# Own buffers for the memory's raw weights, and new durations for transfers, ScalarE and GpSimd in the list scheduler

## The chip, the cores and the metric

The kernel runs on one core of a Trainium2 chip. Five engines of that core run their own instruction streams in order: TensorE (matrix products, called PE in the profile, with its weight loads as PEld), VectorE (DVE), ScalarE (ACT), GpSimd (POOL) and SyncE (SP). In this kernel every transfer between the chip's main memory and the on-chip memory (SBUF) is issued from SP's queue, and is then carried out by 16 transfer engines. Products land in PSUM, which has 8 banks; VectorE and ScalarE read them from there. The metric is the device time of one execution in microseconds, lower is better.

## The reference

One inference step of one layer of a streaming encoder, for 1024 prompt rows and 32 sample rows, width 1024, all in 32-bit floats:

- p = RMSNorm(x) @ w_in. Half of the columns feed an HGRN2 mixer (4 heads, a gated linear recurrence computed in blocks), the other half an RWKV-7 mixer (8 heads, a delta-rule recurrence computed in chunks of 64).
- x = x + concat(HGRN2, RWKV7) @ w_out.
- Cross attention: the memory (256 rows) is normalised and turned into keys and values, mk = RMSNorm(mem) @ w_ck and mv = RMSNorm(mem) @ w_cv, which are also outputs. The sample rows use cached keys and values instead. x = x + softmax(q mk^T / 16) mv @ w_co, with q from w_cq.
- x = x + (silu(n @ w_ff1) * (n @ w_ff3)) @ w_ff2 with 2816 hidden columns, and a last RMSNorm.

Outputs are the normalised rows, the new recurrence states, the last projected rows, and the memory's keys and values.

## The kernel before

The kernel is written in two layers. Class Net calls operations on a recorder (class Graph). Each call becomes a node with an engine, a price in microseconds, predecessors, and the tiles (class Buf) it touches; runs of matmuls up to a cut form one node. Then Graph.order (line 376) is a list scheduler that runs while the program is being built: it keeps a clock for every engine, takes again and again the node that can start first, prefers on one engine the node with the longest remaining path, and gives every new tile an address. The order it finds is what each engine then runs, in order, on the chip. All instructions are emitted from line 365, which is why the profile shows one line for all of them, and tiles there carry the name of the memory region they were put in.

Prices come from `price` (line 218): a duration, which occupies the engine, and a second value, `late`, which delays the successors only. For a transfer the duration occupies SP in the plan.

The SBUF is cut into regions (line 59), counted in units of 66 floats a partition: f0 (192 units), wr (32), r0 (256), rw (64), mb (192) and ma (64). Regions mb and ma change from plain 32-bit tiles to tiles of rounded parts once few enough mixer nodes are left. HOME (line 64) binds some tile classes to regions; a plain class that is not in HOME may go to any plain region but wr, and its tile is given out only if a reserve of units stays free (RESERVE, line 61; 32 units for phase 1). FIFO (line 69) limits how many tiles of a class live at one time, and tiles of a class in FIFO are handed out in program order.

Every matrix product against weights is done with both operands split into a rounded high part and a low remainder. `load_w` (line 764) loads the raw weights with one transfer of 512 KB, casts the high part on ScalarE, subtracts on VectorE or GpSimd for the low part, and three products follow for each block. Its raw tile is of class "wr" (2 alive, region wr), high and low parts are of classes "wh" and "wl" (2 alive each, region rw).

Work is in phases: 0 the two mixers with their projections, 1 the memory's keys and values (`memory_kv`, line 886), 2 the output projection, 3 cross attention, 4 the hidden layer of the feed-forward part, 5 and 6 its output and the last norm. LEAD (line 63) says how many nodes of earlier phases may be left when a phase starts; it is 1100 for phase 1. Phase 1 has the lowest priority of all (bias of 2e5 on the path), so that it fills gaps. It loads 16 half weights of 512 rows by 256 columns, 8 of w_ck and 8 of w_cv, and each one serves 24 products of 256 columns: 2 row tiles, 4 blocks, 3 products. The normalised memory rows lie in region ma, so that in the profile these products read "rw,ma".

Of the kernel before, what the change touches and what calls it, by code (L numbers as in the profile page):

```python
# [11 lines left out]
F32 = mybir.dt.float32  # L12
# [4 lines left out]
ALU = mybir.AluOpType  # L17
# [48 lines left out]
        "ac": ("f0", "ma"), "hst2": ("f0", "ma"), "fu": ("f0", "ma")}  # L66

TASTE = [{"f0": 0.0, "wr": 0.0, "r0": 0.0, "rw": 0.0, "mb": 20.0, "ma": 10.0}, {"f0": 20.0, "wr": 0.0, "r0": 0.0, "rw": 0.0, "mb": 0.0, "ma": 10.0}]
FIFO = {"wr": 2, "wh": 2, "wl": 2, "p": 44, "rp": 5, "op": 32, "sr": 2, "sh": 4, "sx": 4, "sh3": 8, "hst2": 4, "xr": 2, "wr2": 4, "wh2": 8, "wl2": 8, "ckv": 7, "mrow": 2}

INDEX = (np.arange(128, dtype=np.int64)[:, None] << 20) + np.arange(8 * 1056, dtype=np.int64)[None]

# [145 lines left out]
def price(eng, method, args, kw):  # L218

    out = args[0] if args else kw.get("out")  # L220
    n = math.prod(out.shape[1:]) if out is not None and hasattr(out, "shape") else 1
    if method == "dma_start":
        return max(0.4, n * out.shape[0] * 4 / 200e3), 1.9
    if eng == "tensor":
        if method == "transpose":
            return (0.056 if args[1].shape[0] <= 64 else 0.109), 0.0
        lhs = kw["lhsT"]
        k, m = lhs.shape[0], math.prod(lhs.shape[1:])
        if lhs.dtype == F16:
            return max(0.029, n / 2400 + 0.002), 0.0  # L230
        if lhs.dtype == F32R:
            return (n if n >= 256 else 4 * n) * 0.4375e-3 + 0.007, 0.0
        if k <= 64 and m <= 64:
            return max(0.03, n * 0.92e-3), 0.0
        if k <= 64:
            return max(0.112, n * 1.25e-3), 0.0
        if m <= 64:
            return (0.059 if n >= 64 else 0.112), 0.0
        return max(0.223, n / 600 + 0.005), 0.0
    if eng == "vector":  # L240
        if method == "tensor_reduce":
            n = math.prod(args[1].shape[1:])
        if method == "tensor_tensor_scan":
            return 0.07 + n * 2.08e-3, 0.0
        return 0.065 + n * 1.05e-3 + (0.065 if method == "scalar_tensor_tensor" else 0.0), 0.0
    if method == "preload_act_table_set":
        return 1.28, 0.0
    if eng == "scalar":
        pointer = any(isinstance(kw.get(k), View) for k in ("scale", "bias", "accum_out"))
        return (0.18 if args[1].buf.space == "PS" else 0.21) + n * 0.83e-3 + (0.095 if pointer else 0.0), 0.0  # L250
    if method == "affine_select":
        return 0.35, 0.0
    if method == "memset":
        return 0.06 + n * 0.5e-3, 0.0
    if method == "tensor_tensor":
        return 0.13 + n * 2.12e-3 + (0.45 if args[3] == ALU.pow else 0.0), 0.0
    if method == "tensor_scalar":
        return 0.3 + n * (2.9e-3 if args[4] == ALU.max else 1.3e-3), 0.0
    return 0.24 + n * 1e-3, 0.0


def shares_port(eng, method, args):
# [22 lines left out]
class Graph:  # L285
    def __init__(self, ctx, tc):
# [5 lines left out]
        for name in ("vector", "scalar", "gpsimd", "tensor", "sync"):  # L292
            setattr(self, name, Engine(self, name))
        self.bufs = {c: [] for c in FIFO}

# [26 lines left out]
    def record(self, eng, method, args, kw):  # L322
        if eng == "tensor" and self.open is not None:
            node = self.open
        else:
            node = Node(self, eng)
        self.open = node if eng == "tensor" else None
        cost, late = price(eng, method, args, kw)
        node.port = shares_port(eng, method, args)
        node.cost, node.late = node.cost + cost, max(node.late, late)  # L330
        node.calls.append((method, args, kw))
        node.dense = method == "matmul" and kw["lhsT"].dtype == F32R
        for at, a in list(enumerate(args)) + list(kw.items()):
            if isinstance(a, View):
                a.buf.touch(node, a, at in (0, "out", "accum_out"))
        if method == "activation" and args[2] in (AF.Exp, AF.Ln, AF.Tanh, AF.Sigmoid):
            if self.fence is not None:
                node.preds[self.fence] = None
            self.table.append(node)
        if method == "preload_act_table_set":  # L340
            node.preds.update(dict.fromkeys(self.table))
            self.fence = node
        return node
# [32 lines left out]
    def order(self):  # L376
# [84 lines left out]
        banks = [0.0] * 8  # L461
        turn, live = dict.fromkeys(FIFO, 0), dict.fromkeys(FIFO, 0)
        done, oldest, out = set(), 0, []
# [26 lines left out]
        def fits(n, start):  # L490
# [7 lines left out]
            if not new:  # L498
                return start
            for c in FIFO:  # L500
                k = sorted(b.turn for b in new if b.cls == c)
                if k and (k != list(range(turn[c], turn[c] + len(k))) or live[c] + len(k) > FIFO[c]):
                    return None
# [19 lines left out]
        def take(n, start):  # L523
            for b in sorted((b for b in n.bufs if b.at is None and b.fixed is None), key=lambda b: -b.units):
# [8 lines left out]
                freed[b.at:b.at + b.units] = BIG  # L533
                if b.cls in FIFO:
                    turn[b.cls] += 1
# [9 lines left out]
        while len(done) < len(nodes):  # L545
# [48 lines left out]
            for b in n.bufs:  # L594
                b.left -= 1
                if not b.left and b.fixed is None:
# [3 lines left out]
                    else:  # L600
                        freed[b.at:b.at + b.units] = end + FREE_SB
                        if b.cls in FIFO:
                            live[b.cls] -= 1
# [16 lines left out]
class Net:  # L620
# [140 lines left out]
        return self.par[:, at + j:at + j + n]  # L761


    def load_w(self, ap, nk, gain=None, m=128, small=False, eng=None):

        nc = self.nc
        size, tag = (nk, "2") if small else (1024 // m, "")
        raw = self.wp.tile([128, size, m], F32, tag="wr" + tag, name="wraw")[:, :nk]
        nc.sync.dma_start(raw, ap.rearrange("(k p) m -> p k m", p=128))
        hi = self.wp.tile([128, size, m], F32R, tag="wh" + tag, name="whi")[:, :nk]  # L770
        if gain is not None:
            nc.vector.tensor_tensor(raw, raw, gain.unsqueeze(2).to_broadcast([128, nk, m]), ALU.mult)
        nc.scalar.copy(hi, raw)
        lo = self.wp.tile([128, size, m], F32R, tag="wl" + tag, name="wlo")[:, :nk]
        (eng or nc.vector).tensor_tensor(lo, raw, hi.bitcast(F32), ALU.subtract)
        return hi, lo
# [109 lines left out]
    def memory_kv(self):  # L886

        nc = self.nc
        mh = self.ap.tile([128, KD, 256], F32R, name="mh")
        ml = self.ap.tile([128, KD, 256], F32R, name="ml")  # L890
        rs = self.load_rows([(self.i["mem_prompt"][0, 128 * a:128 * a + 128, :], 128, 128 * a) for a in range(2)], mh, ml, None,
                            lambda: self.ap.tile([128, 512], F32, tag="mrow", name="mrow"), self.P("g_mem", 0, KD))
        for h in range(4):
            for key, out in (("w_ck", self.mk), ("w_cv", self.mv)):
                pss = [self.psg.tile([128, 256], F32, tag="g", name="ps_mem") for _ in range(2)]
                for a in range(2):
                    hi, lo = self.load_w(self.i[key][0, 512 * a:512 * a + 512, 256 * h:256 * h + 256], 4, m=256,
                                         eng=nc.vector)
                    for t, ps in enumerate(pss):
                        ts = slice(128 * t, 128 * t + 128)  # L900
                        nc.cut()
                        for k in range(4):
                            mm = partial(nc.tensor.matmul, ps)
                            mm(lhsT=mh[:, 4 * a + k, ts], rhs=hi[:, k], start=a + k == 0, stop=False)
                            mm(lhsT=mh[:, 4 * a + k, ts], rhs=lo[:, k], start=False, stop=False)
                            mm(lhsT=ml[:, 4 * a + k, ts], rhs=hi[:, k], start=False, stop=a == 1 and k == 3)
                for t, ps in enumerate(pss):
                    nat = self.ap.tile([128, 256], F32, tag="nat", name="nat")
                    nc.scalar.activation(nat, ps, AF.Copy, scale=rs[:, t:t + 1])
                    nc.sync.dma_start(out[:, t, h], nat)  # L910
# [982 lines left out]
```

## Time and profile before

| | us |
|---|---|
| median of 3 runs | 1973.01 |
| lowest and highest run | 1971.82, 1973.35 |
| span of the profiled execution, first to last instruction | 1970.2 |
| TensorE busy in it | 1873.7 |
| VectorE busy | 1403.0 |
| ScalarE busy | 837.8 |
| GpSimd busy | 657.9 |

The page shows busy time of each engine, then 40 slices of the span with the busy share in tenths, the granted TensorE clock in tenths, and the busy share of the transfer engines. A timeline row has start, length, engine, line, operation, out<-in by region, shape and count, and in brackets the idle time before it with what ended that. "DMA f<-out_dram" as a releaser means that the engine waited for that transfer to land. A row of SPq is the issue of a transfer, not its duration.

### The profile page before, as it was taken

How to read it: one execution, taken by the hardware profiler on the slowest of the kernel's cores; microseconds unless marked ns; L12 is line 12 of the kernel's file. 1: busy time of each engine (PE TensorE's matmuls, PEld its weight loads, DVE VectorE, ACT ScalarE, POOL GpSimd, SP SyncE). 2: the span in 40 equal slices, each digit the busy share in tenths (PEclk: the TensorE clock that was granted, in tenths of full speed). 3: DMA queues.
4: the chain of work that ended last, by engine and by line, in shares of the span. 5: the costliest groups of instructions: out<-in, count | busy, mean ns of one | idle time of the engine just before them, and what ended most of it. 6: DMA issues, size and time to landing. Idle time of an engine off the chain costs nothing. (4 is left out here: it accounts for less than half of the span.)

```text
span 1970.2 us, 40636 instructions
## 1 busy us (share of the span) xinstructions
PE 1873.7 (95%) x15785; PEld 1733.5 (88%) x15785; DVE 1403.0 (71%) x3112; ACT 837.8 (43%) x2151; POOL 657.9 (33%) x926
## 2 busy tenths in 40 slices
PE   6899999999999999799999999899999999999998
PEld 6788888887888888699899999799999999999997
DVE  4787789568957876524555446797777877968997
ACT  4553545454545455533322235533323323464432
POOL 4632444235425432104500003633332333322421
PEclk8899999999999999799999999899999999999999
DMA  4100110011001102551112112222223224455632
GB/s 143 38 7 26 41 40 23 7 50 38 13 28 45 34 18 69 155 156 43 43 43 70 39 60 88 71 82 93 82 100 129 88 83 137 138 181 170 183 90 89
DMA packets 158111, 149.51 MB, mean 76 GB/s; under 512 B 10080, under 2 KB 146400, under 8 KB 157920
## 3 DMA queue, kind: packets, MB, share of 16 engines
q1 hardware_dynamic: 157920, 146.93, 23.7%
q8 instruction: 124, 2.03, 0.4%
q14 instruction: 67, 0.55, 0.1%
HBM read 111.02 MB, written 35.88 MB: 75 GB/s over the span
## 5 line engine op out<-in xcount | busy, mean ns | idle before, releaser
L365 PE MATMUL bank<-r,rw 128*128 128x264 f32 (+1 forms) x5808 | 928.4, 310 | 28.8 <-DVE rw L365 10.6
L365 PEld LDWEIGHTS bank<-r,rw 128*128 128x128 f32 x5808 | 824.6, 190 | 49.1 <-DVE rw L365 12.2
L365 PE MATMUL bank<-mb,rw 128*128 128x264 f32 (+3 forms) x3456 | 484.5, 293 | 10.4 <-DVE rw L365 8.9
L365 PEld LDWEIGHTS bank<-mb,rw 128*128 128x128 f32 x3456 | 455.5, 189 | 19.5 <-DVE rw L365 13.5
L365 DVE TENSOR_TENSOR f<-bank,f 128x264 f32<-128x264 f32 (+11 forms) x798 | 317.5, 421 | 121.2 <-PE bank L365 114.9
L365 PE MATMUL bank<-f 64*64 64x64 f32 (+8 forms) x2472 | 281.6, 258 | 36.1 <-DVE f L365 17.5
L365 PEld LDWEIGHTS bank<-f 64*64 64x64 f32 (+5 forms) x1675 | 169.3, 157 | 73.0 <-DVE f L365 22.4
L365 ACT CAST rw<-wr 128x1024 fp32r<-128x1024 f32 (+3 forms) x183 | 132.8, 730 | 224.7 <-PE bank L365 138.7
L365 POOL TENSOR_TENSOR f<-f 128x2 f32<-128x2 f32 (+9 forms) x167 | 106.2, 648 | 317.3 <-ACT f L365 241.0
L365 ACT ACTIVATE f<-f 128x256 f32<-128x256 f32 (+7 forms) x392 | 158.0, 423 | 114.1 <-DVE f L365 88.1
L365 DVE TENSOR_TENSOR f<-f 128x264 f32<-128x264 f32 (+10 forms) x266 | 187.7, 719 | 24.3 <-POOL f L365 12.0
L365 DVE TENSOR_TENSOR rw<-wr,rw 128x512 fp32r<-128x512 f32 (+3 forms) x153 | 129.4, 850 | 81.4 <-ACT rw L365 80.6
L365 ACT COPY f<-bank 128x264 f32<-128x264 f32 (+6 forms) x251 | 87.6, 361 | 119.1 <-PE bank L365 104.6
L365 ACT CAST rw<-ma 128x512 fp32r<-128x512 f32 (+2 forms) x124 | 70.9, 573 | 153.2 <-POOL ma L365 85.8
L365 DVE TENSOR_TENSOR rw<-ma,rw 128x512 fp32r<-128x512 f32 (+2 forms) x124 | 82.5, 672 | 35.2 <-ACT rw L365 35.0
L365 POOL TENSOR_SCALAR f<-f 128x64 f32<-128x64 f32 (+6 forms) x117 | 49.2, 422 | 165.0 <-DVE f L365 104.7
L365 PE MATMUL bank<-f,mb 64*64 64x64 f32 (+9 forms) x982 | 84.5, 241 | 3.8 <-DVE f L365 2.4
L365 ACT ACTIVATE f<-bank,f 128x256 f32<-128x256 f32 (+4 forms) x127 | 52.6, 430 | 73.8 <-DVE f L365 32.4
L365 ACT CAST f<-bank 128x256 f16<-128x256 f32 (+1 forms) x144 | 46.5, 339 | 87.8 <-PE bank L365 56.9
L365 POOL TENSOR_TENSOR ma<-ma 128x512 f32<-128x512 f32 (+4 forms) x41 | 53.4, 1304 | 90.5 <-DVE rw L365 90.1
L365 POOL TENSOR_TENSOR ma<-wr 128x512 f32<-128x512 f32 (+1 forms) x13 | 25.1, 1928 | 161.6 <-DVE rw L365 95.2
L365 DVE TENSOR_TENSOR f<-bank,r 128x264 f32<-128x264 f32 (+1 forms) x56 | 25.2, 465 | 71.2 <-PE bank L365 64.2
(189 smaller groups left out, 2233.2 us busy)
## 6 DMA issues: line engine op xcount, KB each, us to landing
wr<-in_w_in_dram SPq DMA_DIRECT2D x30, 512.0 KB
wr<-in_w_ff_dram SPq DMA_DIRECT2D x27, 512.0 KB
ma<-in_w_ff_dram SPq DMA_DIRECT2D x25, 512.0 KB
h_scratch<-f SPq DMA_DIRECT2D x18, 528.0 KB
f<-h_scratch SPq DMA_DIRECT2D x36, 264.0 KB
ma<-h_scratch SPq DMA_DIRECT2D x34, 264.0 KB
h_scratch<-f SPq DMA_DIRECT2D x12, 396.0 KB
f<-mix_scratch SPq DMA_DIRECT2D x24, 176.0 KB
```

The lines of the kernel that those rows point to most:

```text
L365: getattr(eng, method)(*args, **kw)
```

## The change

The raw tiles of the memory's weights become a class of their own, "wm", with up to 6 alive; "wm" is not in HOME. Class "wr" keeps its 2 tiles for all other weights. The high and low parts stay in "wh" and "wl". In `price`, the duration of a transfer falls from bytes/200e3 to bytes/330e3 us (its `late` of 1.9 stays), ScalarE's fixed part falls from 0.18 (source in PSUM) and 0.21 (source in SBUF) to 0.06 and 0.11 while it gets a `late` of 0.1, and GpSimd's prices of affine_select, memset, tensor_scalar and the remaining operations change. Prices of TensorE, VectorE and GpSimd's tensor_tensor stay.

```diff
-FIFO = {"wr": 2, "wh": 2, "wl": 2, "p": 44, "rp": 5, ...
+FIFO = {"wm": 6, "wr": 2, "wh": 2, "wl": 2, "p": 44, "rp": 5, ...
...
     if method == "dma_start":
-        return max(0.4, n * out.shape[0] * 4 / 200e3), 1.9
+        return max(0.4, n * out.shape[0] * 4 / 330e3), 1.9
...
-        return (0.18 if args[1].buf.space == "PS" else 0.21) + n * 0.83e-3 + (0.095 if pointer else 0.0), 0.0
+        return (0.06 if args[1].buf.space == "PS" else 0.11) + n * 0.83e-3 + (0.095 if pointer else 0.0), 0.1
     if method == "affine_select":
-        return 0.35, 0.0
+        return 0.38, 0.0
     if method == "memset":
-        return 0.06 + n * 0.5e-3, 0.0
+        return 0.1 + n * 0.8e-3, 0.0
     if method == "tensor_tensor":
         return 0.13 + n * 2.12e-3 + (0.45 if args[3] == ALU.pow else 0.0), 0.0
     if method == "tensor_scalar":
-        return 0.3 + n * (2.9e-3 if args[4] == ALU.max else 1.3e-3), 0.0
-    return 0.24 + n * 1e-3, 0.0
+        return 0.2 + n * (3.4e-3 if args[4] == ALU.max else 1.05e-3), 0.0
+    return 0.16 + n * 1e-3, 0.0
...
-    def load_w(self, ap, nk, gain=None, m=128, small=False, eng=None):
+    def load_w(self, ap, nk, gain=None, m=128, small=False, eng=None, early=False):
...
-        raw = self.wp.tile([128, size, m], F32, tag="wr" + tag, name="wraw")[:, :nk]
+        raw = self.wp.tile([128, size, m], F32, tag="wm" if early else "wr" + tag, name="wraw")[:, :nk]
...
                     hi, lo = self.load_w(self.i[key][0, 512 * a:512 * a + 512, 256 * h:256 * h + 256], 4, m=256,
-                                         eng=nc.vector)
+                                         eng=nc.vector, early=True)
```

More of the change, by code (lines that the diff above doesn't have):

```diff
@@ L68 @@
 TASTE = [{"f0": 0.0, "wr": 0.0, "r0": 0.0, "rw": 0.0, "mb": 20.0, "ma": 10.0}, {"f0": 20.0, "wr": 0.0, "r0": 0.0, "rw": 0.0, "mb": 0.0, "ma": 10.0}]
-FIFO = {"wr": 2, "wh": 2, "wl": 2, "p": 44, "rp": 5, "op": 32, "sr": 2, "sh": 4, "sx": 4, "sh3": 8, "hst2": 4, "xr": 2, "wr2": 4, "wh2": 8, "wl2": 8, "ckv": 7, "mrow": 2}
+FIFO = {"wm": 6, "wr": 2, "wh": 2, "wl": 2, "p": 44, "rp": 5, "op": 32, "sr": 2, "sh": 4, "sx": 4, "sh3": 8, "hst2": 4, "xr": 2, "wr2": 4, "wh2": 8, "wl2": 8, "ckv": 7, "mrow": 2}
 INDEX = (np.arange(128, dtype=np.int64)[:, None] << 20) + np.arange(8 * 1056, dtype=np.int64)[None]
```

## The prediction

> **What bounds the kernel now.** I read the page's busy shares and slices first, then busy time by stage, then the timeline of the one weak stage engine by engine, and last the group rows for prices.
>
> ```profile
> span 1970.2 us, 40636 instructions
> PE 1873.7 (95%) x15785; PEld 1733.5 (88%) x15785; DVE 1403.0 (71%) x3112; ACT 837.8 (43%) x2151; POOL 657.9 (33%) x926
> PE   6899999999999999799999999899999999999998
> PEclk8899999999999999799999999899999999999999
> DMA  4100110011001102551112112222223224455632
> ```
>
> TensorE is the bound: 1970.2 - 1873.7 leaves 96.5 us without a matmul. The seventeenth slice (788 to 837 us) is the one dent in the middle, for the engine and for its granted clock, and the transfer engines are at their mid-run peak there. The stages, as busy time of each engine, granted clock, transfer share, GB/s:
>
> ```profile
> 0.00:160.00 160.00, 133.06 (x1130) 119.09 (x1131) 110.00 (x246) 81.76 (x205) 79.33 (x172) 0.91 0.21 65
> 160.00:600.00 440.00, 429.00 (x4385) 364.32 (x4383) 327.77 (x910) 220.30 (x683) 172.56 (x331) 1.00 0.10 28
> 600.00:781.00 181.00, 177.75 (x1876) 149.90 (x1873) 130.28 (x386) 89.29 (x289) 69.64 (x128) 1.00 0.12 36
> 781.00:866.00 85.00, 68.25 (x474) 62.19 (x472) 42.55 (x92) 45.07 (x103) 10.30 (x23) 0.86 0.57 178
> 1160.00:1320.00 160.00, 147.29 (x1136) 143.92 (x1136) 117.52 (x218) 76.92 (x180) 62.70 (x58) 0.96 0.26 84
> 1700.00:1850.00 150.00, 143.41 (x1145) 141.52 (x1144) 123.80 (x215) 76.41 (x165) 45.88 (x38) 0.99 0.55 166
> 1850.00:1971.00 121.00, 111.40 (x860) 107.17 (x858) 106.33 (x252) 40.03 (x104) 30.98 (x55) 0.98 0.34 108
> 500.00:550.00 50.00, 47.18 (x570) 39.66 (x569) 43.64 (x115) 22.18 (x67) 21.36 (x42) 1.00 0.04 13
> ```
>
> The 85 us in which the last mixer head ends and the memory keys and values are made lose 85 - 68.25 = 16.75 us. Opened up on TensorE (start, length, tiles, count, idle time before and what ended it):
>
> ```profile
> 786.72 6.26 PE L365 MATMUL bank<-rw,ma 128*128 128x256 f32 x48
> 793.87 9.09 PE L365 MATMUL bank<-f 128*128 128x128 f32 x59 [0.89 <-DVE f L365]
> 805.15 0.28 PE L365 MATMUL bank<-f 128*32 128x128 f32 x1 [2.18 <-DVE f L365]
> 806.06 2.98 PE L365 MATMUL bank<-f 128*32 128x32 f32 x10 [0.63 <-DVE f L365]
> 810.56 0.31 PE L365 MATMUL bank<-f 32*128 32x32 f32 x1 [1.52 <-ACT f L365]
> 810.80 14.40 PE L365 MATMUL bank<-rw,ma 128*128 128x256 f32 x96
> 830.25 1.11 PE L365 MATMUL bank<-f 128*128 128x128 f32 x4 [5.05 <-DMA f<-out_dram]
> 834.74 0.58 PE L365 MATMUL bank<-rw,ma 128*128 128x256 f32 x1 [3.38 <-ACT rw L365]
> 836.00 17.05 PE L365 MATMUL bank<-rw,ma 128*128 128x256 f32 x120 [0.68 <-DVE rw L365]
> 853.93 5.95 PE L365 MATMUL bank<-rw,ma 128*128 128x256 f32 x48 [0.88 <-DVE rw L365]
> ```
>
> The rows "rw,ma" are the memory products, 24 to one loaded half weight. They are meant as filler for the mixers' last dependent steps, but three halves are eaten by 793 and the fourth is not there until 810.8, so 0.89, 2.18, 0.63 and 1.52 us (5.22) stay open. Then 5.05 and 3.38 (8.43) wait on transfers. What the transfer queue and ScalarE did meanwhile:
>
> ```profile
> 787.18 0.38 SPq L365 DMA_DIRECT2D wr<-in_w_cv_dram  x1
> 792.40 0.43 SPq L365 DMA_DIRECT2D wr<-in_w_ck_dram  x1
> 815.19 10.76 SPq L365 DMA_DIRECT2D f<-mix_scratch  x12
> 826.00 0.42 SPq L365 DMA_DIRECT2D f<-out_dram  x1
> 826.47 0.46 SPq L365 DMA_DIRECT2D wr<-in_w_cv_dram  x1
> 853.90 0.39 SPq L365 DMA_DIRECT2D wr<-in_w_cv_dram  x1
> ...
> 833.64 1.04 ACT L365 CAST rw<-wr 128x1024 fp32r<-128x1024 f32 x1 [1.66 <-DMA wr<-in_w_cv_dram]
> 857.88 1.05 ACT L365 CAST rw<-wr 128x1024 fp32r<-128x1024 f32 x1 [3.03 <-DMA wr<-in_w_cv_dram]
> ```
>
> With two raw buffers the next half is asked for only when an earlier one has been split, and then stands behind twelve reads of the mixers' output: asked for at 826.47, cast at 833.64, 7.2 us. In the quieter stretch it is 857.88 - 853.90 = 4.0 us.
>
> **The change part by part.**
>
> Buffers. Six raw halves hold 6 x 24 products; 48 products take 5.95 us warm (853.93), so they cover 17.9 us, against a longest wait of 7.2 us. The 16 loads stay 16, each a 0.4 us issue; they only move forward on SP, past reads and writes of the mixers' scratch. The 3.38 us is a wait for exactly such a load and goes. The 5.05 us is for a cached-key read at the tail of the same burst; with the memory halves already in place, the planner has products to run before it, so I take it back too: 8.43 us. Of the 5.22 us I take half, 2.6: the raw halves will be there, but their high and low parts still have two buffers each, handed out in program order after those of the projections, and casts must slip between the mixers' own ScalarE steps. Late next are these casts and the VectorE subtractions: the 0.68 and 0.88 us stay.
>
> Clock. 96 products from 810.80 take 14.40 us where the warm rate gives 96 x 5.95/48 = 11.9, and the 120 from 836.00 take 17.05 instead of 14.9: 2.5 and 2.2 us are slow clock after idling (granted 0.86 over the stage). I take back the 2.2 and half of the 2.5: 3.4. The Trainium skill, "TensorE: Matmul & The Clock Gate", Part 1, says that the clock halves only after an idle window of some 3.4 us and then needs one as long of steady work. By that rule remaining waits under a microsecond trip nothing and all 4.7 come back, 1.3 more than I take; the slow start at 810.8 came after several waits of at most 2.2, so the trace does not quite agree.
>
> Space. A raw half is 1024 floats a partition, 16 units. The old pair lay in a region of its own; the new class is bound to none, so it takes up to 96 of the 192 units of f0, where the mixers hold their work. Phase 1 may start with 1100 mixer nodes left. If a page comes free late, its load waits on SP, and every projection load and scratch write queued behind waits as well. The bound is a stretch that lost space before:
>
> ```profile
> 615.95 0.32 SPq L365 DMA_DIRECT2D mix_scratch<-ma  x1
> ...
> 783.83 1.04 ACT L365 CAST rw<-wr 128x1024 fp32r<-128x1024 f32 x1
> 784.78 0.48 ACT L365 CAST mb<-f 128x352 fp32r<-128x352 f32 x1
> ```
>
> 615.95 is the last mixer transfer from region ma; its 64 units then go to the memory rows, and yet TensorE is 177.75/181 = 98.2% busy from 600 to 781, against 429/440 = 97.5% before. Space for four raw halves was worth nothing there. I take 1 us of cost; the ends stand below.
>
> Prices. These move no instruction by themselves; they change the order in which a greedy list scheduler places all of them. ScalarE: the 1024-column cast starts at 783.83, the next instruction at 784.78, 0.95 later; the new price is 0.11 + 0.85 = 0.96 with 0.1 of tail, the old 1.06 without. So the plan stops overcharging about 0.1 us on each of 2151 instructions. Transfers: 512 KB were priced 2.62 + 1.9 = 4.5 us and are now 1.59 + 1.9 = 3.5; the trace's 4.0 and 7.2 lie above that. GpSimd moves by a tenth or two either way. Where ScalarE looked full, the plan may now place casts earlier: 1160 to 1320 loses 160 - 147.29 = 12.7 us, and of that I take 2. Nothing in the trace shows the new order, so its cost is bounded: below nothing, by the 43 us idle outside the start (26.9), the memory stage (16.75) and the end (9.6); above, by every mixer stretch from 160 to 781 becoming like its worst, 500 to 550 (2.82/50 = 5.6% idle against 14.25/621 = 2.3%): 3.3% of 621 = 20 us. I take +2, near zero, because most stretches are within 3% of full under the old order and new prices of the same size cannot win much there.
>
> Sum: 8.4 + 2.6 + 3.4 + 2 - 1 - 2 = 13.4. The profiled execution spans 1970.2; the three runs lie 1.6 to 3.2 above that, the median 2.8. 1970.2 - 13.4 + 2.8 = 1959.6; I say 1959.5.
>
> **Rivals.**
>
> A. It does only part of what it says: raw halves land early, but casts keep their turn, so the 5.22 us stay, and the 5.05 us stays because it waits for a cached-key read. Gain 3.38 + 2.2 = 5.6: 1967.4. For it: two buffers for the high and low parts, untouched. Against: those two keep TensorE fed from 836.
>
> B. Transfers planned too short; this one ends slower. In the feed-forward output stage the order counts on 264 KB reads after 0.82 + 1.9 = 2.7 us (old 3.3), and the chain shows one that took
>
> ```profile
> 1722.42 0.52 SPq L365
> 1722.99 3.24 DMA ma<-h_scratch
> ...
> 1726.21 0.39 PE L365 MATMUL bank<-r,rw 128*128 128x264 f32 x1 [2.89 <-ACT r L365]
> ...
> f<-h_scratch SPq DMA_DIRECT2D x36, 264.0 KB
> ma<-h_scratch SPq DMA_DIRECT2D x34, 264.0 KB
> ```
>
> 0.52 + 3.24 = 3.8, behind which TensorE stood 2.89. An order made for 2.7 puts its casts ahead of other ready work on ScalarE, and TensorE waits behind them. The stage carries 166 GB/s, so reads are late there all the time. Each such place costs up to 2.89; five eat the gain, eight (23 us) give 1959.5 + 23 = 1982.5. Against it: there are 70 such reads, the old 3.3 was below 3.8 as well, and yet all idle time of TensorE from 1700 to 1850 is 150 - 143.41 = 6.6 us. The Trainium skill, "DMA: Bandwidth & Descriptors", Latency and other measured facts, gives memory access 0.2 us on average and 2 at high load. By that rule the new price is right in the mixers and 1.8 short here, which is this rival; the 4.0 and 7.2 us above agree with it in kind.
>
> C. The mixers lose their order, for want of f0 or by the new prices: at their worst stretch throughout, +20 - 3 already taken: 1976.5. Against: the ma row above.
>
> **How the numbers follow.** Forecast 0.58, A 0.14, B 0.16, C 0.12. The forecast's own range is 1950 to 1967. The low end, 1943, is all 16.75 + 4.7 of the memory stage and 8 of the 12.7; the high end, 1981, stops just short of B's eight places. A difference under 0.2% (4 us) can't be told from none. Faster: the forecast and A, less 0.04 at their upper edge: 0.68. Within 0.2%: most of that and half of C (1976.5 is 3.5 above the median): 0.09. Slower: B, the other half of C and 0.01: 0.23.
>
> **What would show it.** Right: memory loads named after a tile other than wr, the first ones before 781; no wait of TensorE on a memory load; 781 to 866 shorter by 10 us or more, its clock above 0.95; 12 us or less idle from 1160 to 1320. Wrong: casts of memory halves bunched after 809 as now (A); more idle time with h_scratch or weight transfers behind it after 1160 (B); 160 to 781 longer by over 5 us, or SP queued on memory loads there (C).

## The result, and the profile after

The changed kernel is slower: 1983.47 us (median of 4 runs, 1980.12 to 1984.8) against 1972.41 for the kernel before beside it, ratio 1.0061 with a 95% interval of 1.0046 to 1.0077. The prediction said 1959.5. The profiled execution spans 1981.6 us, 11.4 more than before.

First the page of the changed kernel: span, busy time of the engines, TensorE's busy tenths in 40 slices, and the granted clock in tenths.

```profile
span 1981.6 us, 40552 instructions
PE 1883.0 (95%) x15785; PEld 1741.0 (88%) x15785; DVE 1414.6 (71%) x3112; ACT 821.7 (41%) x2150; POOL 655.4 (33%) x926
PE   7999999999999999799899999699999999999998
PEclk9899999999999999899999999799999999999999
```

The products are the same 15785, yet TensorE is busy 1883.0 - 1873.7 = 9.3 us longer, and 2.1 of the 11.4 us are more idle time (98.6 against 96.5). The 9.3 us fit a slower clock: the mean granted clock of the profiled execution is 0.976 where it was 0.981, and 1873.7 x 0.981/0.976 = 1883.3. The dent in the seventeenth slice is still there, and the shallow one in the twenty-sixth (1238 to 1288 us), 8 tenths before, is now the deepest with 6; its clock went from 8 tenths to 7.

Busy time of each engine by stage, in the columns the prediction used, for the changed kernel:

```profile
0.00:160.00 160.00, 140.72 (x1267) 124.65 (x1268) 119.06 (x267) 83.18 (x217) 86.22 (x177) 0.95 0.21 65
160.00:600.00 440.00, 421.26 (x4127) 357.33 (x4125) 319.77 (x862) 201.95 (x653) 168.90 (x318) 0.97 0.10 28
600.00:781.00 181.00, 177.04 (x1904) 146.47 (x1904) 128.80 (x382) 82.25 (x268) 70.02 (x132) 1.00 0.08 25
781.00:866.00 85.00, 73.86 (x531) 69.17 (x530) 50.18 (x119) 53.31 (x137) 14.76 (x29) 0.90 0.64 203
1160.00:1320.00 160.00, 142.75 (x1087) 139.01 (x1087) 108.46 (x206) 74.19 (x176) 60.73 (x59) 0.93 0.22 68
1700.00:1850.00 150.00, 143.97 (x1155) 142.31 (x1154) 122.25 (x204) 77.41 (x167) 44.33 (x36) 0.99 0.53 166
```

Every stage moved, those that have nothing to do with the memory too. The start is better (140.72 busy against 133.06). The mixers lose: idle time from 160 to 781 is 18.74 + 3.96 = 22.7 us where it was 14.25, and the clock from 160 to 600 fell from 1.00 to 0.97, which makes some 12 us of slower products (an estimate, 421.26 x 0.03). Summed from the start, 7298 products are done by 781 us where 7391 were. The memory stage idles 11.1 where it was 16.75. The stretch from 1160 to 1320, with the first block of the feed-forward part, idles 17.25 where it was 12.71.

Fixed windows mix a shift with a loss, so here are three places of the program that both kernels reach: the start of the cross attention, the second block of the hidden layer, and the last transposes. TensorE's timeline, before:

```profile
966.99 8.18 PE L365 MATMUL bank<-r,rw 128*128 128x352 f32 x41 [4.08 <-DVE rw L365]
...
1303.93 7.41 PE L365 MATMUL bank<-mb,rw 128*128 128x264 f32 x46 [2.70 <-DVE rw L365]
...
1960.75 0.99 PE L365 MATMUL bank<-f 128*128 128x128 f32 x7 [0.89 <-DVE f L365]
```

and after:

```profile
970.39 4.83 PE L365 MATMUL bank<-r,rw 128*128 128x352 f32 x19 [4.97 <-DVE rw L365]
...
1316.40 3.79 PE L365 MATMUL bank<-mb,rw 128*128 128x264 f32 x29 [1.82 <-DVE rw L365]
...
1972.28 0.44 PE L365 MATMUL bank<-f 128*128 128x128 f32 x2 [0.88 <-DVE f L365]
```

Up to the cross attention 3.4 us are lost, from there to the second hidden block 12.5 - 3.4 = 9.1, and afterwards 1.0 is won back (11.5 at the end). The prediction had -11.4 for the first stretch (buffers, clock, space, reordering) and -2 for the second.

What happened in the memory stage, TensorE's timeline after:

```profile
782.53 11.75 PE L365 MATMUL bank<-r,rw 128*128 128x352 f32 x72
794.11 1.03 PE L365 MATMUL bank<-f 128*128 128x128 f32 x8
801.94 7.41 PE L365 MATMUL bank<-f 128*128 128x128 f32 x32 [6.79 <-DVE f L365]
810.53 0.66 PE L365 MATMUL bank<-f 128*128 128x128 f32 x4 [1.18 <-DMA f<-in_mem_prompt_dram]
...
822.37 1.84 PE L365 MATMUL bank<-rw,ma 128*128 128x256 f32 x12
824.14 0.24 PE L365 MATMUL bank<-f 32*128 32x32 f32 x1
824.32 13.17 PE L365 MATMUL bank<-rw,ma 128*128 128x256 f32 x109
838.74 15.77 PE L365 MATMUL bank<-rw,ma 128*128 128x256 f32 x131 [1.25 <-DVE rw L365]
```

The first memory product ("rw,ma") runs at 822.37. Before, the first was

```profile
781.85 3.00 PE L365 MATMUL bank<-rw,ma 128*128 128x256 f32 x24
```

By 822 the mixers' tail is all but over: its dependent steps had nothing beside them, and TensorE stood 6.79 us in one piece. The queue of SP shows why: the first memory weight is asked for only at

```profile
815.13 0.38 SPq L365 DMA_DIRECT2D f<-in_w_ck_dram  x1
...
816.11 0.44 SPq L365 DMA_DIRECT2D f<-in_w_ck_dram  x1
```

and before at

```profile
702.82 0.41 SPq L365 DMA_DIRECT2D wr<-in_w_ck_dram  x1
```

The change that was to bring the weights earlier brought them 112 us later. The memory's own rows, which every memory product needs as well, came late too. They are read in four transfers, and the last of them is issued after the change at

```profile
807.36 0.38 SPq L365 DMA_DIRECT2D f<-in_mem_prompt_dram  x1
```

and before, together with the third, at

```profile
754.09 0.94 SPq L365 DMA_DIRECT2D f<-in_mem_prompt_dram  x2
```

The wait of 1.18 us at 810.53 is for these rows. So weights that came early would probably have filled the gap only in part; no run shows that. Once both are there, the stage runs as hoped: from 822 to 1000 TensorE waits for VectorE (7.1 us in all) and once for ScalarE (0.7), and for no transfer.

TensorE's waits summed by what ended them (us in all, times, longest), before:

```profile
PE bank L365 <- DVE rw L365: 21.5, 23, 4.1
PE bank L365 <- DVE f L365: 20.5, 27, 3.6
PE bank L365 <- ACT rw L365: 7.1, 4, 3.4
PE bank L365 <- DMA f<-out_dram: 5.0, 1, 5.0
```

and after:

```profile
PE bank L365 <- DVE f L365: 27.2, 26, 6.8
PE bank L365 <- DVE rw L365: 27.1, 22, 6.0
PE bank L365 <- ACT rw L365: 2.2, 2, 1.7
```

The two waits that the change was predicted to remove, 3.38 of the 7.1 us and the 5.0, did go, and longer waits for VectorE came in their place.

### The profile page after: what moved, and what is told of

Its sections match the earlier page's. It is cut to its first block, busy times and chain, and to the rows that moved or that the text cites. A ratio compares the mean times of both kernels' runs of the same rounds, so it can differ in the third digit from the quotient of the medians.

```text
span 1981.6 us, 40552 instructions
## 1 busy us (share of the span) xinstructions
PE 1883.0 (95%) x15785; PEld 1741.0 (88%) x15785; DVE 1414.6 (71%) x3112; ACT 821.7 (41%) x2150; POOL 655.4 (33%) x926
## 5 line engine op out<-in xcount | busy, mean ns | idle before, releaser
L365 PE MATMUL bank<-mb,rw 128*128 128x264 f32 (+4 forms) x3432 | 477.9, 293 | 8.7 <-DVE rw L365 8.5
L365 DVE TENSOR_TENSOR f<-bank,f 128x264 f32<-128x264 f32 (+9 forms) x783 | 309.3, 421 | 129.1 <-PE bank L365 125.2
L365 PE MATMUL bank<-f 64*64 64x64 f32 (+7 forms) x2496 | 286.4, 260 | 35.2 <-DVE f L365 18.2
L365 PEld LDWEIGHTS bank<-f 128*128 128x128 f32 (+4 forms) x1692 | 173.5, 161 | 73.7 <-DVE f L365 26.4
L365 ACT CAST rw<-wr 128x512 fp32r<-128x512 f32 (+3 forms) x172 | 118.3, 691 | 213.6 <-PE bank L365 124.7
L365 POOL TENSOR_TENSOR f<-f 128x264 f32<-128x264 f32 (+8 forms) x154 | 102.7, 678 | 298.7 <-ACT f L365 236.6
L365 DVE TENSOR_TENSOR f<-f 128x264 f32<-128x264 f32 (+8 forms) x255 | 171.6, 690 | 14.6 <-ACT f L365 6.8
L365 PE MATMUL bank<-f,mb 64*128 64x64 f32 (+9 forms) x865 | 77.3, 244 | 4.7 <-DVE f L365 3.8
L365 POOL TENSOR_TENSOR rw<-wr,rw 128x1024 fp32r<-128x1024 f32 x30 | 71.3, 2382 | 20.2 <-ACT rw L365 10.3
L365 DVE TENSOR_TENSOR rw<-f,rw 128x512 fp32r<-128x512 f32 (+3 forms) x61 | 53.1, 871 | 31.4 <-ACT rw L365 29.1
```

The source lines that it names most:

```text
L365: getattr(eng, method)(*args, **kw)
```

## The experiments

The expectations name their theories by letters. P, later V: the new prices themselves are worse for the order; T and A are the parts of it for transfers and for ScalarE. N: any edit of a price redraws the order of everything, by lot; in its first form, every new order is worse than the one of before. S, for the class: raw tiles that may lie only in f0 come late, because f0 has no room for them. M: the class helps by itself. Each ratio is against the kernel before in the same series, whose medians lie between 1971.14 and 1972.77; all kernels compute the whole reference.

**One half of the change at a time.** The class alone, old prices:

```diff
-FIFO = {"wr": 2, "wh": 2, ...
+FIFO = {"wm": 6, "wr": 2, "wh": 2, ...
...
+        raw = self.wp.tile([128, size, m], F32, tag="wm" if early else "wr" + tag, name="wraw")[:, :nk]
```

> The class of own buffers alone, with all old prices. Theory S (space: a raw half now needs one whole free page of 16 units in f0, where the mixers scatter tiles of 4 units, so it is loaded late): the first memory weight load comes after 750 us as in the changed kernel (815.13; before 702.82), the first memory product after 800, and the kernel loses part of the 11.4 us. Theory P (the prices cost the time): memory loads are late or not, but the kernel stays within 4 us of 1972.4. Theory N (any new order of this scheduler is worse than the one of before): 1976 to 1985 whatever the memory stage does.

Measured 1961.83, ratio 0.9961 (0.9948 to 0.9973). None of the three theories had that. Of S only the late load came true (758.04 us): the first memory product ran at 783.96, not after 800, and the kernel gained. Up to 781 us the class alone leaves the order nearly as it was (from 160 to 600 TensorE is busy 428.89 us with 4368 products, before 429.00 with 4385). All new prices, with the old class:

```diff
-        raw = self.wp.tile([128, size, m], F32, tag="wm" if early else "wr" + tag, name="wraw")[:, :nk]
+        raw = self.wp.tile([128, size, m], F32, tag="wr" + tag, name="wraw")[:, :nk]
```

> All new prices, raw halves in the old class with two buffers. Theory S: first memory weight load near 703 as before, products again serve as filler before 794, and the kernel is back within 4 us of 1972.4. Theory P: the loss stays, 1978 to 1986, with the stretch of the first hidden block (1237 to 1316 in the changed kernel) idle as in the changed kernel. Theory N: 1976 to 1985.

Measured 1988.04, ratio 1.0088 (1.0073 to 1.0103): 16.8 us slower than before. That is above all three ranges, by 2 us for P, whose sign it has. So under the old prices the class is a gain of 9.4 us, and under the new ones it takes 4.6 off a loss of 16.8. In this pair of halves the loss is the prices'.

**A price changed by nothing.** The kernel before, with the price of a transfer off by half a per cent:

```diff
-        return max(0.4, n * out.shape[0] * 4 / 200e3), 1.9
+        return max(0.4, n * out.shape[0] * 4 / 201e3), 1.9
```

> The kernel before with one price nudged without any meaning: a transfer's bytes are divided by 201e3 instead of 200e3, 0.5%. Theories S and P: 1972.4 within 4 us, because nothing that matters moved. Theory N: the order is drawn anew and the time lies 4 to 15 us above 1972.4.

Measured 1976.19, ratio 1.0027 (1.0014 to 1.0040): 4.9 us above the kernel before beside it, clear of the noise, but 3.8 above the 1972.4 of the expectation, just on the side of S and P. And ScalarE's fixed part off by 2 ns:

```diff
-        return (0.18 if args[1].buf.space == "PS" else 0.21) + ...
+        return (0.182 if args[1].buf.space == "PS" else 0.212) + ...
```

> A second nudge without meaning: ScalarE's fixed price 0.182 and 0.212 instead of 0.18 and 0.21, 1%. Theory N: again 3 to 15 us above 1971, with another stage hit than with the first nudge. If the order of before is nothing special: on either side of 1971, within 5 us.

Measured 1998.41, ratio 1.0134 (1.0109 to 1.0159): 25.6 us for 2 ns an instruction, more than the 3 to 15 that N expected. The program pays in several places: TensorE idles 4.4 us more before 160, 6.6 more from 160 to 600 and 6.5 more from 781 to 866. The page of this kernel:

```profile
span 1998.1 us, 40602 instructions
PE   6898999998999999779999999899999999999998
PEclk8998999999999999789999999899999999999999
```

Slices four and ten have new dents, and the seventeenth and eighteenth are both deep. The same two nudges on the changed kernel:

```diff
-        return max(0.4, n * out.shape[0] * 4 / 330e3), 1.9
+        return max(0.4, n * out.shape[0] * 4 / 331e3), 1.9
```

> The changed kernel with another such nudge: transfers at 331e3 instead of 330e3. Theory V: 1979 to 1988. Theory N: 1962 to 1990.

Measured 1993.22, ratio 1.0110 (1.0088 to 1.0131).

```diff
-        return (0.06 if args[1].buf.space == "PS" else 0.11) + ...
+        return (0.062 if args[1].buf.space == "PS" else 0.112) + ...
```

> The changed kernel with a nudge without meaning: ScalarE's fixed price 0.062 and 0.112 instead of 0.06 and 0.11. Theory V (the new prices are worse in themselves: orders made with them lie around 1983): 1979 to 1988. Theory N (prices only redraw the order; with own buffers the six draws so far run from 1961.8 to 1987.2): 1962 to 1990, and together with the next run as likely below 1979 as above.

Measured 1977.95, ratio 1.0028 (1.0017 to 1.0039). V's 1979 to 1988 missed both, one on each side; N's 1962 to 1990 missed the first by 3 us. Edits that mean nothing move the kernel by +4.9, +25.6, +9.8 and -5.5 us (the last two against 1983.47). The whole result, +11, is of that size. That speaks for theory N as far as the size goes; that no rule is behind the draws isn't shown. A worse order by the new prices as such (V) isn't shown either, and the sample is too small to exclude it.

**One price at a time.** Transfers alone:

```diff
+        return max(0.4, n * out.shape[0] * 4 / 330e3), 1.9
```

> The kernel before with the new price of transfers alone (330e3 instead of 200e3). All new prices together, without own buffers, cost 16.8 us (1988.04 against 1971.25), lost between 250 and 470 us in the mixers. Theory T (the cheaper transfer is what hurts): 1982 to 1990, and the granted clock in the stretches 200 to 350 and 450 to 500 falls below 1.00 as with all prices. Theory A (ScalarE's cheaper issue is what hurts): within 6 us of 1971. Theory N (any new order costs some 5 us, as the meaningless nudge did): 1974 to 1980.

Measured 1973.96, ratio 1.0004 (0.9993 to 1.0015), no difference, so T is out. ScalarE alone:

```diff
+        return (0.06 if args[1].buf.space == "PS" else 0.11) + n * 0.83e-3 + (0.095 if pointer else 0.0), 0.1
```

> The kernel before with ScalarE's new price alone (0.06 and 0.11 with 0.1 of tail instead of 0.18 and 0.21). Theory A: 1982 to 1990 with the mixers' stretch 250 to 470 longer by 10 us or more. Theory T: within 6 us of 1971. Theory N: 1974 to 1980.

Measured 2008.90, ratio 1.0192 (1.0168 to 1.0216). GpSimd alone:

```diff
+        return 0.38, 0.0
...
+        return 0.1 + n * 0.8e-3, 0.0
...
+        return 0.2 + n * (3.4e-3 if args[4] == ALU.max else 1.05e-3), 0.0
+    return 0.16 + n * 1e-3, 0.0
```

> The kernel before with GpSimd's new prices alone. If GpSimd's prices hurt: 1980 or more. Theories A and T: within 6 us of 1971. Theory N: 1974 to 1980.

Measured 2008.69, ratio 1.0186 (1.0164 to 1.0209). Alone, two of the three cost 36 us each, far above A's range of 1982 to 1990; all three together cost 16.8. Parts that don't add up are not effects of single prices that could be summed. They read as draws again, the largest so far.

**The class under every set of prices.** If each order is a draw, one pair says little on the class. So it was put beside each of the other price sets, the edit of the class being the one shown first. With the transfer's nudge:

```diff
+FIFO = {"wm": 6, "wr": 2, ...
...
+        return max(0.4, n * out.shape[0] * 4 / 201e3), 1.9
```

> Own buffers on top of the meaningless transfer nudge, which alone took 1976.2. Theory M: 1964 to 1972. Theory N: 1962 to 2009 without regard to 1976.

Measured 1986.94, ratio 1.0083 (1.0065 to 1.0101). With ScalarE's nudge:

```diff
+FIFO = {"wm": 6, "wr": 2, ...
...
+        return (0.182 if args[1].buf.space == "PS" else 0.212) + ...
```

> Own buffers on top of the meaningless ScalarE nudge, which alone took 1998.4. Theory M (own buffers help by themselves, because raw halves no longer stall the memory stage): 1978 to 1990, with TensorE's waits on ScalarE's weight casts (19.0 us under the nudge alone) below 8. Theory N (every edit only redraws the order, own buffers too): anywhere from 1962 to 2009, as likely above 1998 as below it.

Measured 1975.62, ratio 1.0022 (1.0011 to 1.0033). With the new price of transfers:

```diff
+FIFO = {"wm": 6, "wr": 2, ...
...
+        return max(0.4, n * out.shape[0] * 4 / 330e3), 1.9
```

> Own buffers with the new price of transfers, which alone took 1974.0. Theory M: 1962 to 1970. Theory N: 1962 to 2009, most likely above 1974.

Measured 1978.06, ratio 1.0038 (1.0025 to 1.0050). With ScalarE's new price:

```diff
+FIFO = {"wm": 6, "wr": 2, ...
...
+        return (0.06 if args[1].buf.space == "PS" else 0.11) + n * 0.83e-3 + (0.095 if pointer else 0.0), 0.1
```

> Own buffers with ScalarE's new price alone; without own buffers that price took 2008.9. Theory M (own buffers help most where the memory stage is worst): 1980 to 1995. Theory N: 1962 to 1990 too, but then without a smaller wait of TensorE on the casts of weights than the 14.3 us of that price alone.

Measured 2029.29, ratio 1.0290 (1.0273 to 1.0307), the slowest of all. With GpSimd's new prices:

```diff
+FIFO = {"wm": 6, "wr": 2, ...
...
+        return 0.2 + n * (3.4e-3 if args[4] == ALU.max else 1.05e-3), 0.0
+    return 0.16 + n * 1e-3, 0.0
```

> Own buffers with GpSimd's new prices, which alone took 2008.7. Theory M: 1988 to 2000. Theory N: 1962 to 2009, about the mean of the draws so far (1985) more likely than 2009.

Measured 1987.17, ratio 1.0078 (1.0056 to 1.0100). The seven pairs, in the order of how much later the first memory load is issued with the class than without it (starts in SP's timeline, medians in us):

| prices | first load, old class | first load, own class | later by | time, old class | time, own class | difference |
|---|---|---|---|---|---|---|
| ScalarE nudged | 733.0 | 762.1 | 29 | 1998.41 | 1975.62 | -22.8 |
| old | 702.8 | 758.0 | 55 | 1971.25 | 1961.83 | -9.4 |
| GpSimd new | 726.9 | 782.4 | 56 | 2008.69 | 1987.17 | -21.5 |
| transfers new | 712.0 | 797.6 | 86 | 1973.96 | 1978.06 | +4.1 |
| all new (the change) | 719.3 | 815.1 | 96 | 1988.04 | 1983.47 | -4.6 |
| transfers nudged | 704.9 | 808.8 | 104 | 1976.19 | 1986.94 | +10.8 |
| ScalarE new | 713.0 | 839.5 | 127 | 2008.90 | 2029.29 | +20.4 |

In all seven the load comes later, never earlier. The mean difference in time is -3.3 us, with both signs: no gain to rely on. None of M's five ranges was met; N's, which are wide, held four times, and 2029.29 lies outside both. But the differences follow the delay almost in order: up to 56 us later the class pays, from 86 on it mostly costs. That was read off after the runs and is a relation in seven pairs, with no run that moves the load and nothing else.

**Where the raw tile may lie.** The changed kernel with two raw tiles bound to a larger region wr, taken from f0:

```diff
-REGIONS = {"f0": (192, "left", "FFFFFFF", ()), "wr": (32, "left", "FFFFFFF", ()), ...
+REGIONS = {"f0": (160, "left", "FFFFFFF", ()), "wr": (64, "left", "FFFFFFF", ()), ...
...
+HOME = {"wm": ("wr",), ...
...
-FIFO = {"wm": 6, ...
+FIFO = {"wm": 2, ...
```

> The changed kernel, but the raw halves get two pages bound to them: region wr grows from 32 to 64 units, f0 shrinks from 192 to 160, class wm has 2 tiles in wr. Theory S: the first memory loads come before 700 us, memory products fill the 6.79 us gap at 794, and the kernel gains 5 to 12 us on the changed one (1972 to 1978), unless the smaller f0 slows the mixers. Theory P: loads come early and the time stays within 4 us of 1983.5. Theory N: anywhere from 1974 to 1990.

Measured 1974.48, ratio 1.0022 (1.0008 to 1.0035), 9.0 us below the changed kernel. SP's timeline of it:

```profile
626.48 0.98 SPq L365 DMA_DIRECT2D wr<-in_w_ck_dram  x2
```

With a place of their own the first two loads are issued 189 us earlier than in the changed kernel, as S had it, and memory products run from 786.98 on, in the place of the old gap; the time lies in the ranges of S and of N, so it doesn't part them. Nor was it the early loads alone: the memory's rows are read from 756.31 on, so the two raw tiles lay there unused until then, and f0 and the number of tiles changed as well. Three things can keep the raw tiles out of f0: 32 units must stay free beside the tile (RESERVE); or the tile, 16 units, needs one whole free page of 16, while the mixers scatter tiles of 4 over the pages (function `place` looks at pages of 16 units); or f0 is simply so full that fewer than 16 units are free at all. The reserve can be taken away alone, under the new prices and under the old:

```diff
-RESERVE = [64, 32, 24, 24, 24, 24, 24]
+RESERVE = [64, 0, 24, 24, 24, 24, 24]
```

> The changed kernel with the reserve of phase 1 set from 32 units to 0, so that a raw tile of the memory, 16 units in f0, needs only a place and no spare space beside it. What is read is the start of the first memory load: 815.1 us in the changed kernel, 719.3 us in the kernel with the same prices and the old class. If the reserve held the loads back, the first one comes at 740 or before. If the want of one whole free page of 16 units held them back, it stays after 780. The time says little, since this is one more redrawing of the order: by the spread of those so far, anywhere from 1960 to 2000.

Measured 1978.53, ratio 1.0034 (1.0019 to 1.0049). The first load, in SP's timeline:

```profile
794.70 0.38 SPq L365 DMA_DIRECT2D f<-in_w_ck_dram  x1
```

The same edit with the class and the old prices:

> The own class with the old prices and with the reserve of phase 1 set from 32 units to 0. The first memory load starts at 758.0 us with the reserve and at 702.8 us in the kernel before. If the reserve held the loads back, it comes at 725 or before; if the want of a whole free page, at 745 or later. The time: between 1957 and 1990, as for any other redrawing.

Measured 1980.16, ratio 1.0045 (1.0030 to 1.0059), and the first load:

```profile
788.33 0.38 SPq L365 DMA_DIRECT2D f<-in_w_ck_dram  x1
```

Both stay late, 794.70 and 788.33, the second even 30 us later than with the reserve. So it is not the reserve by itself, though the edit frees it for all of phase 1, the memory's rows among them. The want of a whole page and the plain want of room remain. The kernel with pages of its own fits both; no run freed pages in f0 alone, and the runs don't show which of the two it is, or when.

**A version that beats both.** The class with the old prices, and phase 1 starting later, when 900 nodes of the mixers are left:

```diff
-LEAD = {0: BIG, 1: 1100, 2: 250, 3: 400, 4: 100, 5: 200, 6: 200}
+LEAD = {0: BIG, 1: 900, 2: 250, 3: 400, 4: 100, 5: 200, 6: 200}
```

> Own buffers, old prices, and phase 1 may start with 900 mixer nodes left instead of 1100, so that memory rows take space in f0 later. If own buffers with old prices are a good order because of what they leave free in f0: 1957 to 1964. Theory N: anywhere, most likely above 1970.

Measured 1957.06, ratio 0.9940 (0.9916 to 0.9964), within the expectation's 1957 to 1964. Its timeline of TensorE in the mixers' tail and its busy time from 781 to 866:

```profile
794.70 2.83 PE L365 MATMUL bank<-rw,ma 128*128 128x256 f32 x12
797.37 0.60 PE L365 MATMUL bank<-f 128*128 128x128 f32 x4
797.73 1.67 PE L365 MATMUL bank<-rw,ma 128*128 128x256 f32 x12
...
816.46 3.04 PE L365 MATMUL bank<-f 128*128 128x128 f32 x24
```

```profile
781.00:866.00 85.00, 74.56 (x546) 70.04 (x545) 49.85 (x109) 51.72 (x125) 14.65 (x26) 0.96 0.63 190
```

This is the picture that the prediction had in mind: memory products between the mixers' dependent steps, 10.4 us idle instead of 16.75, the clock at 0.96. Its first load starts at 760.22, no earlier than with the class alone. Being one more draw, it is a good kernel and no proof that 900 is the better number.

## Why the prediction was wrong, point by point

The bound was read rightly: TensorE, with the memory stage as its weakest place. The sum failed on two of its steps.

**Prices.** The step that failed most. It took a gain of 2 us for better casts and a cost of 2 for a new order, "near zero, because most stretches are within 3% of full under the old order". The prices alone cost 16.8 us; the rest of the miss is the class, which gave 4.6 us under the new prices where 13.4 were added up for it. The bound was wrong as well, +20 at most: ScalarE's price alone cost 36 and, with the class, 58. The flaw is in the argument: a stretch that is 97% full shows how good this one order is, not how good a neighbouring order would be. A change of 2 ns in one price gave +25.6. Nor were the prices shown to be truer, but for one. ScalarE's was, 0.96 against 0.95 in the trace where the old one said 1.06, and it alone cost 36 us: a truer price did not make a better order. That of a 512 KB transfer went from 4.5 to 3.5 where the trace has 4.0 and 7.2, and that of a 264 KB read from 3.3 to 2.7 where one took 3.8.

**Space.** Taken at 1 us, from a row which showed that four halves' space was worth nothing to the mixers. The question should have been the other way round: not what the mixers lose to the raw tiles, but whether the raw tiles get in among the mixers' tiles at all. They did so 112 us later than the old pair, 96 of them with the prices equal, although the prediction had the loads "only move forward". "The first ones before 781" was the sign to look for, and it came out wrong (815.13). Under the old prices the class was 55 us late, still before 781 (758.04), and gained.

**Buffers.** Half right. The two waits of 8.43 us are gone in the changed kernel. The 2.6 us, half of the small waits in the mixers' tail, had the wrong sign: without filler that tail opened by 6.79 and 1.18. With the class alone the sum of buffers, clock and space was predicted at -13.4 (8.4 + 2.6 + 3.4 less 1), and the run gave -9.4; the size was near, but the memory stage gave only a part of it, 85 - 71.54 = 13.5 us idle against 16.75:

```profile
781.00:866.00 85.00, 71.54 (x516) 67.50 (x515) 48.90 (x102) 49.86 (x114) 9.89 (x23) 0.90 0.61 189
```

**Clock.** Where the waits went, the full rate came: 109 products in 13.17 us and 131 in 15.77 are 0.121 and 0.120 each, against 0.124 in the prediction's warm row. But the new wait of 6.79 us bought a new slow stretch: the 32 products from 801.94 take 7.41 us, 0.23 each, where the same form takes 3.04/24 = 0.127 in the kernel with the later start. The Trainium skill, "TensorE: Matmul & The Clock Gate", Part 1, lets the clock halve after an idle window of some 3.4 us; here the trace agrees with it. But a wait that long is not needed in this kernel: the mixers' clock fell to 0.97 between 160 and 600, where the longest of TensorE's waits is 2.6 us:

```profile
PE bank L365 <- DVE f L365: 10.6, 10, 2.6
```

The prediction gave the slow clock to the memory stage alone and had no term for the mixers'.

**The rivals.** A did not happen as it was meant. Its sign, memory casts bunched after 809, did show, but because the loads themselves were issued from 815 on, not because casts kept their turn. B did not happen either: the longer waits after 1240 end on VectorE and GpSimd (below), and from 1700 to 1850 TensorE idles 150 - 143.97 = 6.0 us, less than the 6.6 before, so transfers that are planned too short cost nothing there, and the new price of transfers alone gave 1973.96, no difference. That B's 1982.5 lies within 1 us of the result is luck. C, that the mixers lose their order by space or by the new prices, is what happened: its sign was over 5 us lost from 160 to 781, and 8.5 more are idle. It was given 12 in 100 because its two doors, space and prices, were each judged nearly shut from one row. From 160 to 600 TensorE idles 16.8 us at a clock of 0.97 with the prices alone, and 11.1 us at 1.00 with the class alone, as before (11.0): the door was the prices.

**The hidden layer.** Predicted 2 us better, its first block lost 7.9 of the 9.1 us: its first product starts at 1238.37 where it was 1233.80, and the second block at 1316.40 where it was 1303.93. The page's dent at slice twenty-six is three waits of TensorE, in the changed kernel:

```profile
1242.10 16.27 PE L365 MATMUL bank<-r,rw 128*128 128x264 f32 x118 [3.32 <-DVE rw L365]
1261.79 3.89 PE L365 MATMUL bank<-f 128*128 128x352 f32 x6 [3.43 <-POOL f L365]
...
1272.93 7.92 PE L365 MATMUL bank<-r,rw 128*128 128x264 f32 x46 [5.96 <-DVE rw L365]
```

Before, the waits at these three places were 3.16, 0.56 and 0.94 us. The last one is explained below. The 46 products after it take 7.92 us where the same 46 took 5.86: slow clock again.

What stays open is why just these orders are slower, and whether the new prices draw from a worse lot than the old ones. Without the class, the old prices and their two nudges gave 1971, 1976 and 1998, the new ones 1988; with it, the old gave 1962, 1976 and 1987, the new 1983, 1978 and 1993. The means with the class are 1975 and 1985, but the ranges overlap, and three draws each can't part them.

## What to carry to other kernels

Where a list scheduler orders the whole program, an edit of one price is a new order and not a small change: nudge the same price by a per cent, before and after, and take the spread of these kernels as the resolution with which any such edit can be judged. More buffers help only if their tiles can be placed when they are wanted, so look up what a new tile competes with (region, page size, reserve, and how full it is), and read the start of the first load in the transfer queue before counting the gain. A better order may be kept wherever it is found, as the kernel at 1957 us was, but then as a find and not as a rule.

## What the runs showed of the hardware that was not expected

In one place VectorE was held far longer than its own instruction takes. In the changed kernel one VectorE operation with both inputs in SBUF spans

```profile
1266.16 6.12 DVE L365 TENSOR_TENSOR f<-f 128x352 f32<-128x352 f32 x1
```

while GpSimd, in the last of three operations when it starts, runs without a pause

```profile
1264.32 2.16 POOL L365 TENSOR_TENSOR f<-f 128x264 f32<-128x264 f32 x3
1266.43 1.27 POOL L365 TENSOR_TENSOR ma<-ma,f 128x512 f32<-128x512 f32 x1
1267.66 4.24 POOL L365 TENSOR_TENSOR mb<-f,mb 128x264 fp32r<-128x264 f32 x6
```

and VectorE's ends 0.4 us after the last of these does (1271.90). The group of six such operations, busy time and mean ns, before:

```profile
L365 DVE TENSOR_TENSOR f<-f 128x352 f32<-128x352 f32 x6 | 3.5, 590 | 3.3 <-ACT f L365 3.3
```

and after:

```profile
L365 DVE TENSOR_TENSOR f<-f 128x352 f32<-128x352 f32 x6 | 8.6, 1453 | 3.3 <-ACT f L365 3.3
```

The subtraction that makes a low part of weights stood behind it on VectorE, and TensorE waited 5.96 us for that. The Trainium skill, "SBUF — State Buffer", "SBUF: two separate sides", says that of a VectorE instruction with two SBUF inputs and a GpSimd instruction that reads SBUF, the later one blocks until the first is through. The trace agrees in kind, but here the wait lasted through the rest of the one under way and seven more GpSimd instructions. It is the only wait of this length in the profile of the changed kernel; the next longest VectorE operation in it took 2.7 us.
